# Layer 1 attention on one core: a head's 1280 scores taken in one piece instead of three

## The chip, the core and the metric

The kernel runs on one core of a Trainium2 chip. The metric is the device time of one execution in microseconds (us); the time of a kernel is the median of its timed runs. Engine names are those of the profile: PE is the matrix engine, DVE the vector engine, ACT the scalar engine, POOL and SP the two that mostly issue transfers here. Each engine runs its own instructions strictly in the order of the program and waits where an operand or a buffer is not ready.

## The reference

A two-layer network with a mixer and an expert layer in each layer. The change lies in the mixer of layer 1, in the dense attention of eight heads: 1024 query rows (8 tiles of 128) against 1280 keys (1024 of the sequence, 256 of a context).

```
def gqa_attend(q, k, v, mask, sink, scale):
    s = jnp.einsum('bqhgd,bkhd->bhgqk', q, k).astype(jnp.float32) * scale
    ...
    p = jax.nn.softmax(s, axis=-1)
    ...
    return jnp.einsum('bhgqk,bkhd->bqhgd', p.astype(v.dtype), v)
```

Behind the attention come an output projection (`y_lat`), the residual, a router (softmax over 16 experts for each token) and `lax.top_k(..., cap)` with cap = 128: each expert takes the 128 tokens with the highest router value. Then the experts run over the tokens gathered by these indices.

## The kernel before, in words

Every float32 operand of a matmul is split into a high and a low float16 part, and a product is three matmuls (`mm3`). The attention of layer 1 has 64 units of work, called heads below: 8 query tiles `t` times 8 heads `h`, taken in that order.

For each head `score(t, h, i)` writes the scores in three pieces `i` of 512, 512 and 256 keys (`KB`), three matmuls each, into a PSUM tile `sps` of one bank; five such banks rotate. DVE takes each piece's maximum (L1202). After the third piece DVE joins the three maxima and scales the result to `nm` (L1208, L1209). Then for each piece ACT forms the exponential `pr` with its row sum (L1218) and the high part (L112), and DVE the low part (L114); `pr` has two buffers. The parts are turned by a transposing transfer on SP's queue (`pT<-ps`, L147), the first piece by itself and the other two together. `values()` multiplies the turned parts with `vS` into `po`, thirty matmuls a head; after a tile's eighth head DVE divides by the row sums (`oc`, L1249) and the result is split and turned to `oT`.

Scores are taken `LA = 3` heads ahead of the values. Five streams are woven at build time by costs that each `yield` gives: `att_all` (this attention), `q_all` (the queries of the next tile), `tails`, `choose` and `splits`. A scheduler then fixes the order of every engine's instructions before the program runs; nothing is reordered on the chip.

`tails` first runs the convolution branch (`conv_all`, 576 matmuls into `cvps`) and the scaling of the output weights, and then, for each query tile whose `oT` is done, a tail: 48 matmuls into `yps`, two residual additions on DVE (`xx<-yps`, L301), a norm, eight transposes, sixteen router matmuls with a softmax, and a copy of the router values to `aff` (L334). A tail that is written after `att_all` has ended takes other PSUM tiles (`K["z"]`), which lie where the attention's stood.

`choose` waits for the fifth tail, then takes the 128 highest of the first 640 tokens for all experts at once in 16 rounds of three DVE instructions (`tkvr`, L350, L352, L354, 640 wide). After the eighth tail it does the same for the other 384 tokens (`tkvl`), merges both lists and writes `idxl` (L385), by which POOL gathers the experts' tokens.

Of the kernel before, what the change touches and what calls it, by code (L numbers as in the profile page):

```python
# [11 lines left out]
F32 = mybir.dt.float32  # L12
F16 = mybir.dt.float16
# [3 lines left out]
AF = mybir.ActivationFunctionType  # L17
OP = mybir.AluOpType
AX = mybir.AxisListType
# [3 lines left out]
P = 128  # L23
# [12 lines left out]
IS = 1.0 / WS  # L36
EPS = 1e-6
SC0 = 64.0 ** -0.5
SC1 = 96.0 ** -0.5
# [8 lines left out]
GR = ((0,), (1, 2))  # L48
# [29 lines left out]
class Net:  # L78
# [902 lines left out]
    def odd(self, ms, mw, xs, xsc, xd, h2d, W, then):  # L981
# [9 lines left out]
        if True:  # L991
# [109 lines left out]
            KB = ((0, 512), (512, 512), (1024, 256))  # L1101
            SP = ((), (0, 1), (2,))
# [6 lines left out]
            with self.pool("m1zp", PSUM) as pz:  # L1109
# [57 lines left out]
                if True:  # L1167
                    def Q(t):
                        qT = []
                        for i in range(2):  # L1170
# [5 lines left out]
                            S.activation(q, z, AF.Copy, scale=IS)  # L1176
# [14 lines left out]

                    def score(t, h, i):

                        qT, (c0, w) = K[t][h // 4], KB[i]
                        if i == 0:
                            K["mx"] = self.small.tile([P, 3], F32, name="mx3", bufs=3)
                            K["sp"] = []
                        mx, sp = K["mx"], K["sp"]
# [7 lines left out]
                        dn = self.small.tile([P, 3], F32, name="dn3", bufs=3)  # L1206
# [3 lines left out]
                        pTs = []  # L1210
                        for g, parts in enumerate(GR):
                            n = sum(KB[i][1] for i in parts)
                            ps = pt1.tile([P, 2, n], F16, name="ps1", tag=f"ps{g}", bufs=AB[1])
                            o = 0
                            for i in parts:
                                w = KB[i][1]
                                pr = pt1.tile([P, 512], F32, name="pr1", bufs=AB[0])
# [264 lines left out]
```

## Time and profile before

| what | value |
|---|---|
| median of 3 runs | 2640.53 us (2639.13 to 2646.84) |
| the profiled execution | 2632.11 us, of which the span is 2630.0 us |
| busy over the span | PE 89%, DVE 76%, ACT 65% |
| first scores of layer 1 attention | about 1503 us from the span's start |
| last convolution matmuls | about 1733 us |
| last value matmuls, then `oc` of the last tile | 1937.48 us |
| `idxl` written | 2025.36 us |

The profiled execution is 8.4 us below the median of the timed runs. Busy PE means that matmuls were under way, not that the array was at its peak. The layer 1 attention and the convolution beside it reach from 1503 to 1938 us, and the choice of tokens ends at 2026 us; the rest of the span, layer 0 ahead and the experts of layer 1 behind, is not touched by the diff.

### The profile page before, as it was taken

How to read it: one execution, taken by the hardware profiler on the slowest of the kernel's cores; microseconds unless marked ns; L12 is line 12 of the kernel's file. 1: busy time of each engine (PE TensorE's matmuls, PEld its weight loads, DVE VectorE, ACT ScalarE, POOL GpSimd, SP SyncE). 2: the span in 40 equal slices, each digit the busy share in tenths (PEclk: the TensorE clock that was granted, in tenths of full speed). 3: DMA queues.
4: the chain of work that ended last, by engine and by line, in shares of the span. 5: the costliest groups of instructions: out<-in, count | busy, mean ns of one | idle time of the engine just before them, and what ended most of it. 6: DMA issues, size and time to landing. Idle time of an engine off the chain costs nothing. (4 is left out here: it accounts for less than half of the span.)

```text
span 2630.0 us, 48132 instructions
## 1 busy us (share of the span) xinstructions
PE 2329.2 (89%) x19023; PEld 1415.0 (54%) x19023; DVE 1997.7 (76%) x3586; ACT 1696.7 (65%) x2748; POOL 320.6 (12%) x196
## 2 busy tenths in 40 slices
PE   6889998867999999999969999978982999999995
PEld 2335555543877778786836555535541444444442
DVE  5546767787887788777848687788796889888887
ACT  4434666535777787777726466567655777777774
POOL 1000000003111111111310000000025011112120
PEclk9999999877999999999989999989985999999998
DMA  8783555548998989888967577788866899999997
GB/s 321 192 213 84 134 104 116 123 126 312 352 337 324 328 328 325 327 320 300 326 187 203 119 143 143 133 151 184 176 175 272 311 364 395 368 360 367 361 363 274
DMA packets 461705, 660.25 MB, mean 251 GB/s; under 512 B 371083, under 2 KB 371387, under 8 KB 410789
## 3 DMA queue, kind: packets, MB, share of 16 engines
q1 hardware_dynamic: 439894, 582.81, 69.7%
q0 software_dynamic: 21584, 74.37, 9.8%
q8 instruction: 149, 2.44, 0.4%
q14 instruction: 78, 0.64, 0.1%
HBM read 525.82 MB, written 41.94 MB: 216 GB/s over the span
## 5 line engine op out<-in xcount | busy, mean ns | idle before, releaser
L101 DVE SCALAR_TENSOR_TENSOR spl<-raw,spl 128x2048 f16<-128x2048 f32 x369 | 834.6, 2285 | 167.3 <-ACT spl L100 166.5
L100 ACT ACTIVATE spl<-raw 128x2048 f16<-128x2048 f32 x369 | 693.5, 1911 | 166.4 <-DMA raw<-in_w 109.5
L141 PE MATMUL pa<-xsh,spl 128*128 128x160 f16 x1024 | 214.6, 233 | 2.3 <-ACT xsh L112 2.3
L143 PE MATMUL pb<-xsh,spl 128*128 128x160 f16 x1024 | 214.6, 233 | 0.5 <-DVE spl L101 0.5
L142 PE MATMUL pa<-xsl,spl 128*128 128x160 f16 x1024 | 214.7, 233 | 0.3 <-DVE xsl L114 0.3
L143 PE MATMUL pa<-xsh,spl 128*128 128x160 f16 x1024 | 214.7, 233 | 0.0
L142 PE MATMUL pb<-xsl,spl 128*128 128x160 f16 x1024 | 214.6, 233 | 0.0
L141 PE MATMUL pb<-xsh,spl 128*128 128x160 f16 x1024 | 214.5, 233 | 0.0
L141 PEld LDWEIGHTS <-spl 128*128 128x128 f16 x2048 | 200.6, 98 | 8.9 <-issue 8.0
L141 PE MATMUL y<-spl,gh 128*128 128x512 f16 x512 | 195.2, 384 | 9.0 <-ACT gh L112 8.4
L143 PEld LDWEIGHTS <-spl 128*128 128x128 f16 x2048 | 200.8, 98 | 1.1 <-DVE spl L101 0.7
L142 PEld LDWEIGHTS <-spl 128*128 128x128 f16 x2048 | 200.8, 98 | 0.3
L143 PE MATMUL y<-spl,gl 128*128 128x512 f16 x512 | 190.1, 386 | 11.4 <-DVE gl L114 11.3
L142 PE MATMUL y<-spl,gh 128*128 128x512 f16 x512 | 195.6, 382 | 1.8 <-DVE spl L101 1.8
L594 POOL DMA_INDIRECT xd<-ysb,idxl x31 | 113.2, 3652 | 532.3 <-DVE ysb L587 508.2
L1218 ACT ACTIVATE pr<-sps,nm 128x512 f32<-128x512 f32 (+1 forms) x192 | 116.7, 611 | 88.3 <-DVE nm L1209 67.7
L141 PE MATMUL po<-vS,pT 128*128 128x64 f16 x976 | 118.0, 198 | 49.1 <-DMA pT<-ps 32.5
L1201 PE MATMUL sps<-kT,qT 128*128 128x512 f16 (+1 forms) x576 | 134.4, 355 | 12.3 <-ACT pr L1218 11.9
L114 DVE TENSOR_TENSOR ps<-pr,ps 128x512 f16<-128x512 f32 (+1 forms) x192 | 112.2, 595 | 38.9 <-ACT ps L112 38.3
L141 PEld LDWEIGHTS <-pT 128*128 128x128 f16 x976 | 92.1, 101 | 82.8 <-DMA pT<-ps 46.5
L1202 DVE TENSOR_REDUCE mx<-sps 128x1 f32<-128x512 f32 (+1 forms) x192 | 112.8, 595 | 26.2 <-PE sps L1201 24.9
L208 PE MATMUL modps<-mslab,cs 128*2 128x512 f32 x384 | 88.5, 690 | 33.6 <-DMA mslab<-in_mod_w 28.7
(431 smaller groups left out, 5883.8 us busy)
## 6 DMA issues: line engine op xcount, KB each, us to landing
raw<-in_w SPq DMA_DIRECT2D x384, 1024.0 KB, 6.8
mslab<-in_mod_w SPq DMA_DIRECT2D x80, 512.0 KB, 4.8
mslab<-in_mod_w SPq DMA_DIRECT2D x8, 1024.0 KB, 8.2
raw<-in_wz SPq DMA_DIRECT2D x12, 512.0 KB, 6.4
raw<-in_wconv SPq DMA_DIRECT2D x24, 256.0 KB, 3.8
xin<-in_x POOLq DMA_DIRECT2D x8, 512.0 KB, 4.8
raw<-in_ev_wo SPq DMA_DIRECT2D x8, 512.0 KB, 6.9
xres<-in_x POOLq DMA_DIRECT2D x8, 512.0 KB, 5.4
```

What stands on the lines that cost most here:

```text
L100: self.S.activation(hi, raw, AF.Copy, scale=scale)
L101: self.V.scalar_tensor_tensor(lo, raw, scale, hi, op0=OP.mult, op1=OP.subtract)
L114: return self.V.tensor_tensor(lo, src, hi, OP.subtract)
L141: self.T.matmul(ps, lh, rh, start=first, stop=False)
L142: self.T.matmul(ps, lh, rl, start=False, stop=False)
L143: return self.T.matmul(ps, ll, rh, start=False, stop=last).ins
L208: T.matmul(ps[c0:c0 + 2], lhs, slab[:rows, g * 512:(g + 1) * 512], start=False, stop=(k == 8), tile_position=(0, c0))
L594: G.indirect_dma_start(out=xd, out_offset=IOA(ap=lat[0][:, e:e + 1], axis=0), in_=ysb, in_offset=None, compute_op=OP.add)
L1201: T.matmul(ps[:, :w], qT[:, 4 * j + h % 4], kT[:, k, c0:c0 + w], start=j == 0, stop=j == 2)
L1202: V.tensor_reduce(mx[:, i:i + 1], ps[:, :w], axis=AX.X, op=OP.max)
L1218: S.activation(pr[:, :w], sp[i][:, :w], AF.Exp, bias=nm, scale=SC1, accum_out=dn[:, i:i + 1])
```

## The change

The 1280 scores of a head lie side by side in PSUM. One tile of 2560 columns (five banks) holds two heads: even heads take columns 0 to 1279, odd heads 1280 to 2559. The third bank is shared: its first half belongs to the even head, its second half to the odd one. The odd head's pieces are 256, 512 and 512 keys, so that no piece crosses a bank. One DVE instruction takes the maximum over 1280 columns and negates it; the factor `SC1` moves into the copy of the queries. One ACT instruction forms the exponential of 1280 columns with its row sum straight into `rd`, one ACT instruction the high part, one DVE instruction the low part. `pr` becomes one buffer of 1280 columns. Two turns of five blocks each follow once both parts are there. `values()` works in two groups of five blocks, and for each head the attention's stream yields 0.6 three times and 0.3 twice, 2.4 in all, where it was 2.7.

```
-            KB = ((0, 512), (512, 512), (1024, 256))
-            SP = ((), (0, 1), (2,))
+            KB = ((0, 512), (512, 512), (1024, 256)), ((0, 256), (256, 512), (768, 512))
+            SP = (0, 1), (2,)
...
-                            S.activation(q, z, AF.Copy, scale=IS)
+                            S.activation(q, z, AF.Copy, scale=IS * SC1)
...
+                    two = pp.tile([P, 2560], F32, name="sps1")
+
                     def score(t, h, i):
 
-                        qT, (c0, w) = K[t][h // 4], KB[i]
...
-                        ps = pp.tile([P, 512], F32, name="sps1", tag="s", bufs=AB[4])
+                        n = (8 * t + h) % 2
+                        qT, (c0, w) = K[t][h // 4], KB[n][i]
+                        ps = two[:, 1280 * n:1280 * n + 1280]
                         for j, k in enumerate((h, h, 8)):
-                            T.matmul(ps[:, :w], qT[:, 4 * j + h % 4], kT[:, k, c0:c0 + w], start=j == 0, stop=j == 2)
-                        V.tensor_reduce(mx[:, i:i + 1], ps[:, :w], axis=AX.X, op=OP.max)
-                        sp.append(ps)
-                        if i < len(KB) - 1:
+                            T.matmul(ps[:, c0:c0 + w], qT[:, 4 * j + h % 4], kT[:, k, c0:c0 + w], start=j == 0, stop=j == 2)
+                        if i < len(KB[n]) - 1:
                             return
...
                         nm = self.small.tile([P, 1], F32, name="nm1", bufs=3)
-                        V.tensor_reduce(nm, mx, axis=AX.X, op=OP.max)
-                        V.tensor_scalar(nm, nm, -SC1, None, op0=OP.mult)
...
-                                pr = pt1.tile([P, 512], F32, name="pr1", bufs=AB[0])
-                                S.activation(pr[:, :w], sp[i][:, :w], AF.Exp, bias=nm, scale=SC1, accum_out=dn[:, i:i + 1])
-                                self.split_a(pr[:, :w], ps[:, 0, o:o + w], ps[:, 1, o:o + w])
...
+                        V.tensor_reduce(nm, ps, axis=AX.X, op=OP.max, negate=True)
...
-                        V.tensor_reduce(K["rd", t][:, h:h + 1], dn, axis=AX.X, op=OP.add)
+                        pr = pt1.tile([P, 1280], F32, name="pr1", bufs=1)
+                        S.activation(pr, ps, AF.Exp, bias=nm, accum_out=K["rd", t][:, h:h + 1])
+                        pf = pt1.tile([P, 2, 2, 640], F16, name="ps1", bufs=AB[1])
+                        prg = pr.rearrange("p (g c) -> p g c", g=2)
+                        self.split_a(prg, pf[:, :, 0], pf[:, :, 1])
+                        pTs = []
+                        for g in range(2):
+                            pT = pt1.tile([P, 2, 5, P], F16, name="pT1", tag=f"pT{g}", bufs=AB[2])
+                            self.turn(pT.rearrange("p s b c -> p (s b) c"), pf[:, g].rearrange("p s c -> p (s c)"))
+                            pTs.append(pT)
                         K["p", t, h] = pTs
```

The scheduler makes a new order of all that runs in this stage. Up to the first scores of layer 1 the order of every engine is the same in both programs. Line numbers shift: the maximum is L1203, the exponential L1207, the parts L111 and L113, `oc` L1233, `xx<-yps` L300, the copy to `aff` L333 and the first instruction of a top-k round L349 in the changed program.

The first place is DVE in the last heads, with `mx` the maximum, `ps<-pr` the low part of a head (each head with a number of its own). Before:

```order
L1202 TENSOR_REDUCE mx_24770<-sps_24806 128x1
L301 SCALAR_TENSOR_TENSOR xx<-yps,xx 128x512
L1202 TENSOR_REDUCE mx_24770<-sps_24845 128x1
L114 TENSOR_TENSOR ps_24727<-pr_24728,ps_24727 128x512
L1208 TENSOR_REDUCE nm_24851<-mx_24770 128x1
L114 TENSOR_TENSOR ps_24734<-pr_24735,ps_24734 128x512
L1202 TENSOR_REDUCE mx_24900<-sps_24901 128x1
L1209 TENSOR_SCALAR nm_24851<-nm_24851 128x1
```

Here the maxima of the next head (24770, 24900) stand among the low parts of the head ahead of it (24727, 24734). The same place in the changed program, down to the end of the attention:

```order
L1203 TENSOR_REDUCE nm_23493<-sps_18971 128x1
L113 TENSOR_TENSOR ps_23497<-pr_23495,ps_23497 128x2x640
L1203 TENSOR_REDUCE nm_23557<-sps_18971 128x1
L113 TENSOR_TENSOR ps_23561<-pr_23559,ps_23561 128x2x640
L1203 TENSOR_REDUCE nm_23619<-sps_18971 128x1
L1231 RECIPROCAL rd<-rd 128x8
L113 TENSOR_TENSOR ps_23623<-pr_23621,ps_23623 128x2x640
L1233 TENSOR_TENSOR oc<-po_23362,rd 128x512
L113 TENSOR_TENSOR oh<-oc,oh 128x512
L300 SCALAR_TENSOR_TENSOR xx<-yps,xx 128x512 x2
```

Now the low part of a head always stands ahead of the next head's maximum; so it is for 61 of the 63 pairs of neighbours in the whole stage.

On ACT likewise the exponential and the high part of a head (L1207, L111) now alternate with those of the next, one of each.

The second place is DVE where the choice of tokens begins. Before, its first round (`tkvr`) stands among the low parts of the last two heads:

```order
L1202 TENSOR_REDUCE mx_24981<-sps_25018 128x1
L334 COPY aff<-affps 16x128
L1208 TENSOR_REDUCE nm_25024<-mx_24981 128x1
L350 MAX tkvr<-aff 16x8
L114 TENSOR_TENSOR ps_24938<-pr_24939,ps_24938 128x512
L1209 TENSOR_SCALAR nm_25024<-nm_25024 128x1
L114 TENSOR_TENSOR ps_24945<-pr_24946,ps_24945 128x512
L352 MAX_INDEX tkir<-tkvr,aff 16x8
```

After, 26 rows lie between the last head's low part and it, the residual additions of two and a half tails among them:

```order
L126 TENSOR_SCALAR rstdt<-rstt,rsyt 128x1
L300 SCALAR_TENSOR_TENSOR xx<-yps,xx 128x512
L333 COPY aff<-affps 16x128
L349 MAX tkvr<-aff 16x8
L351 MAX_INDEX tkir<-tkvr,aff 16x8
L353 MATCH_REPLACE aff<-tkvr,aff 16x640
L349 MAX tkvr<-aff 16x8
```

The third place is POOL's queue, which writes a tail's rows back (`xd<-xx`, `h<-xx`) and forms the low parts of expert slabs fetched ahead (`spl<-raw`); such a fetch begins when the attention has ended. Before (`xx_24873` is the fifth tail, the two after it the sixth and seventh):

```order
L306 DMA xd1_64<-xx_24873 128x1024
L336 DMA h21_66<-xx_24873 128x1024
L434 TENSOR_TENSOR spl_25666<-raw_25177,spl_25666 128x2048
L306 DMA xd1_64<-xx_25287 128x1024
L434 TENSOR_TENSOR spl_25670<-raw_25179,spl_25670 128x2048
```

After (`xx_23917` is the fifth tail, `xx_24072` the sixth):

```order
L433 TENSOR_TENSOR spl_24451<-raw_23813,spl_24451 128x2048
L305 DMA xd1_64<-xx_23917 128x1024
L433 TENSOR_TENSOR spl_24455<-raw_23815,spl_24455 128x2048
L335 DMA h21_66<-xx_23917 128x1024
L433 TENSOR_TENSOR spl_24459<-raw_23817,spl_24459 128x2048
L305 DMA xd1_64<-xx_24072 128x1024
```

The fifth tail's two writes, ahead of the first slab before, now stand behind the first and the second slab. Its buffer `xx` is the one that the seventh tail loads into, since two buffers take turns.

The fifth tail is the one whose copy to `aff` opens the choice. In PE's order of before, the fifth tail's `yps` matmuls stand ahead of the last value matmuls, and 144 (three tails) behind them; in the changed program 192 (four tails) stand behind them, and 125 of these ahead of the transpose that delivers the fifth tail's router values. The convolution's 576 matmuls end in both programs when 33 heads are scored and 30 to 31 have their values. Between the scores of two neighbouring heads they come in lumps: 0 to 37 of them after the change.

## Rows read from the trace of the kernel before

**Rows 1.** The page's first part: busy us (share of the span), instructions.

```profile
PE 2329.2 (89%) x19023; PEld 1415.0 (54%) x19023; DVE 1997.7 (76%) x3586; ACT 1696.7 (65%) x2748; POOL 320.6 (12%) x196
```

**Rows 2.** Busy time of the engines in three stretches, clock, transfers.

```profile
core 0: us, PE busy (x) PEld busy (x) DVE busy (x) ACT busy (x) POOL busy (x), PEclk, DMA share, GB/s
1503.00:1733.00 230.00, 222.85 (x1926) 122.54 (x1925) 176.41 (x445) 146.16 (x364) 0.00 (x0) 1.00 0.73 138
1733.00:1938.00 205.00, 165.09 (x1628) 98.95 (x1625) 163.90 (x422) 140.84 (x343) 5.33 (x10) 0.91 0.87 172
1938.00:2026.00 88.00, 44.14 (x221) 25.48 (x220) 71.63 (x197) 53.76 (x45) 44.05 (x17) 0.71 0.62 248
```

**Rows 3.** The same stretches, matmuls into `po` alone: PE busy (count), DVE busy, clock.

```profile
1503.00:1733.00 230.00, 45.38 (x955) 2.04 (x3) 1.00 0.73 138
1733.00:1938.00 205.00, 47.61 (x972) 3.25 (x5) 0.91 0.87 172
```

**Rows 4.** DVE from 1895 us: start, us, operation (first round, last division, end of round 16).

```profile
1925.35 0.82 DVE L350 MAX8 tkvr<-aff 16x8 f32<-16x640 f32 x1
...
1937.48 0.69 DVE L1249 TENSOR_TENSOR oc<-po,rd 128x512 f32<-128x512 f32 x1 [0.56 <-PE po L143]
...
1974.39 0.23 DVE L360 TENSOR_SCALAR tkir<-tkir 16x128 f32<-16x128 uint32 x1
```

**Rows 5.** DVE from 1973 us: second top-k, indices.

```profile
1997.64 0.55 DVE L350 MAX8 tkvl<-aff 16x8 f32<-16x384 f32 x1
...
2025.36 0.17 DVE L385 CAST idxl<-slps 128x16 int32<-128x16 f32 x1 [0.49 <-PE slps L384]
```

**Rows 6.** Groups by shape, 1503 to 1938: busy, mean ns, idle ahead, releasers.

```profile
L1202 DVE TENSOR_REDUCE mx<-sps 128x1 f32<-128x512 f32 x128 | 87.2, 684 | 15.6 <-PE sps L1201 14.6
L1218 ACT ACTIVATE pr<-sps,nm 128x512 f32<-128x512 f32 x128 | 86.5, 680 | 70.0 <-DVE nm L1209 67.7 <-DVE ps L114 2.0
L114 DVE TENSOR_TENSOR ps<-pr,ps 128x512 f16<-128x512 f32 x128 | 85.7, 684 | 35.9 <-ACT ps L112 35.6
L112 ACT ACTIVATE ps<-pr 128x512 f16<-128x512 f32 x128 | 75.1, 625 | 0.3
...
L1218 ACT ACTIVATION_READ_ACCUMULATOR pr<-sps,nm 128x1 f32 x192 | 37.6, 196 | 0.0
...
L1218 ACT ACTIVATE pr<-sps,nm 128x256 f32<-128x256 f32 x64 | 30.1, 471 | 18.3 <-DVE ps L114 18.3
L1202 DVE TENSOR_REDUCE mx<-sps 128x1 f32<-128x256 f32 x64 | 26.7, 417 | 10.6 <-PE sps L1201 10.3
L114 DVE TENSOR_TENSOR ps<-pr,ps 128x256 f16<-128x256 f32 x64 | 26.6, 416 | 3.0 <-ACT ps L112 2.7
L112 ACT ACTIVATE ps<-pr 128x256 f16<-128x256 f32 x64 | 26.6, 415 | 1.7
L1208 DVE TENSOR_REDUCE nm<-mx 128x1 f32<-128x3 f32 x64 | 9.4, 148 | 0.4
```

**Rows 7.** The page's groups: the two parts of an expert slab, 2048 wide.

```profile
L101 DVE SCALAR_TENSOR_TENSOR spl<-raw,spl 128x2048 f16<-128x2048 f32 x369 | 834.6, 2285 | 167.3 <-ACT spl L100 166.5
L100 ACT ACTIVATE spl<-raw 128x2048 f16<-128x2048 f32 x369 | 693.5, 1911 | 166.4 <-DMA raw<-in_w 109.5
```

**Rows 8.** DVE and ACT around 1737 us: a hand-over from one to the other.

```profile
1737.25 0.14 DVE L1209 TENSOR_SCALAR nm<-nm 128x1 f32<-128x1 f32 x1
...
1737.43 0.69 ACT L1218 ACTIVATE pr<-sps,nm 128x512 f32<-128x512 f32 x1 [1.03 <-DVE nm L1209]
```

**Rows 9.** Transfers issued from 1733 to 1938: count, us from issue to landing.

```profile
pT<-ps SPq DMA_TRANSPOSE x64, 3.7
```

**Rows 10.** A window in which PE is half idle (columns as in rows 2).

```profile
1755.00:1780.00 25.00, 13.46 (x121) 6.88 (x120) 23.19 (x43) 18.32 (x39) 0.00 (x0) 0.72 0.80 174
```

**Rows 11.** Third stretch of rows 2, matmuls into `yps` alone: PE busy, DVE busy, clock.

```profile
1938.00:2026.00 88.00, 32.66 (x143) 3.95 (x6) 0.71 0.62 248
```

**Rows 12.** POOL from 1900 us: the low part of the second slab fetched ahead.

```profile
1957.02 4.08 POOL L434 TENSOR_TENSOR spl<-raw,spl 128x2048 f16<-128x2048 f32 x1 [2.27 <-ACT spl L433]
```

More of the change, by code (lines that the diff above doesn't have):

```diff
@@ L47 @@
 AB = (2, 2, 3, 0, 5, 1)
-GR = ((0,), (1, 2))
 LA = 3
@@ L1190, in Q @@
                             yield 0.5
+                    two = pp.tile([P, 2560], F32, name="sps1")
                     def score(t, h, i):
-                        qT, (c0, w) = K[t][h // 4], KB[i]
[L1195 to L1198, printed above, removed]
-                        ps = pp.tile([P, 512], F32, name="sps1", tag="s", bufs=AB[4])
+                        n = (8 * t + h) % 2
+                        qT, (c0, w) = K[t][h // 4], KB[n][i]
+                        ps = two[:, 1280 * n:1280 * n + 1280]
@@ L1205, in score @@
                             return
-                        dn = self.small.tile([P, 3], F32, name="dn3", bufs=3)
                         nm = self.small.tile([P, 1], F32, name="nm1", bufs=3)
-                        V.tensor_reduce(nm, mx, axis=AX.X, op=OP.max)
-                        V.tensor_scalar(nm, nm, -SC1, None, op0=OP.mult)
[L1210 to L1216, printed above, removed]
-                                pr = pt1.tile([P, 512], F32, name="pr1", bufs=AB[0])
-                                S.activation(pr[:, :w], sp[i][:, :w], AF.Exp, bias=nm, scale=SC1, accum_out=dn[:, i:i + 1])
-                                self.split_a(pr[:, :w], ps[:, 0, o:o + w], ps[:, 1, o:o + w])
-                                o += w
-                            pT = pt1.tile([P, 2, n // P, P], F16, name="pT1", tag=f"pT{g}", bufs=AB[2])
-                            self.turn(pT.rearrange("p s b c -> p (s b) c"), ps.rearrange("p s c -> p (s c)"))
-                            o = 0
-                            for i in parts:
-                                w = KB[i][1] // P
-                                pTs.append(pT[:, :, o:o + w])
-                                o += w
@@ L1237, in values @@
                         t, h, i, pT = pend.pop(0)
-                        c0, w = KB[i]
                         if (h, i) == (0, 0):
@@ L1241, in values @@
                         po = K["po", t]
-                        for b in range(w // P):
-                            vb, vs = c0 // P + b, slice(h * 64, h * 64 + 64)
+                        for b in range(5):
+                            vb, vs = 5 * i + b, slice(h * 64, h * 64 + 64)
                             self.mm3(po[:, h], pT[:, 0, b], pT[:, 1, b], vS[:, vb, 0, vs], vS[:, vb, 1, vs], vb == 0, vb == 9)
-                        if (h, i) == (7, len(KB) - 1):
+                        if (h, i) == (7, 1):
                             rd = K["rd", t]
@@ L1261, in att_all @@
                             pTs = K.pop(("p", t, h))
-                            for i in range(len(KB)):
+                            for i in range(2):
                                 pend.append((t, h, i, pTs[i]))
```

## The prediction, made before the changed kernel ran

> **What bounds the kernel now.** The whole-kernel shares [rows 1] call no engine full: PE is busy for 89% of the span. So I cut the stage that the change touches into three stretches [rows 2]. From the first scores at 1503 us to the end of the convolution at 1733 us PE is busy 222.85 of 230 us, DVE 176.41 and ACT 146.16: this stretch is PE's, because the convolution fills what the attention leaves free. From 1733 to 1938 us PE is busy 165.09 of 205 us, DVE 163.90, ACT 140.84. There nobody is full, and the time is made of waits between the three engines. The value matmuls count the heads [rows 3]: 955/30 = 31.8 heads in the first stretch, 7.2 us each; 972/30 = 32.4 in the second, 6.3 us each.
>
> The third stretch, 1938 to 2026 us, is another matter. DVE is busy 71.63 of 88 us with the choice of tokens. Its first top-k starts at 1925.35 us, 12 us before the last head's result is divided at 1937.48 us, and ends at 1974.39 us [rows 4], 49 us with what runs in between. The second top-k starts at 1997.64 us, when the eighth tail is through, and the indices stand at 2025.36 us [rows 5], 27.7 us later. So the first top-k is hidden now: it has 23 us to spare before the second needs it.
>
> **The work that goes.** A head's vector work is read by dividing groups by 64 [rows 6]. DVE: maxima (87.2+26.7)/64 = 1.78 us, low parts (85.7+26.6)/64 = 1.76 us, three small operations of 0.15 us, in all 3.98 us. ACT: exponentials (86.5+30.1)/64 = 1.82 us, three reads of the sum 37.6/64 = 0.59 us, high parts (75.1+26.6)/64 = 1.59 us, in all 4.00 us.
>
> No operation on 1280 columns is in the trace. I extend each from its two nearest sizes. The maximum goes from 417 ns at 256 columns to 684 ns at 512, 1.04 ns a column, so 0.684 + 768 x 0.00104 = 1.48 us. The exponential: 0.680 + 768 x 0.00082 = 1.31 us. The low part, from 684 ns at 512 to 2285 ns at 2048 columns [rows 6, 7]: 1.48 us; the high part, from 625 to 1911 ns: 1.27 us. From below, the bound is no fixed cost left at all; from above, three times the pieces now; I take the straight line, since 2048 columns lie on the far side. With one read of the sum at 0.20 us a head costs DVE 2.96 us and ACT 2.78 us. That is 1.0 and 1.2 us less a head, 65 and 78 us over the stage. Matmuls, turned bytes and the 128 turns stay as they are, so PE has the same work.
>
> The Trainium skill's page Perfetto Trace Analysis, section Optimizing Scalar/DVE Operations, says that grouping into larger operations helps when the engine is saturated, and that breaking instructions up can get work done sooner where it is not saturated but makes others wait. By its first half the sum would be that of the faster case below, by its second half this change loses. The trace agrees with the condition of the second half: in the second stretch DVE is at 80% and ACT at 69%, and PE waits.
>
> **The wait that comes.** Before, a head's three pieces let DVE and ACT work on two heads at once. Now the orders shown ahead leave one chain: exponential, high part, low part, the next head's maximum, the next exponential. The single `pr` says the same: its next writer waits for the low part. The chain is 1.31 + 0.20 + 1.27 + 1.48 + 1.48 = 5.74 us a head; hand-overs between engines cost some 0.04 us (0.14 us from 1737.25, then 1737.43 [rows 8]), and neighbours on one engine overlap by as much. PE hides in it: a head's nine score matmuls must wait for the exponential ahead, since both heads share the third bank, but they need only be done by the end of the low part.
>
> The same Trainium skill page, section Matmuls, wants independent matmul groups to rotate through different PSUM banks so that reading one overlaps writing the next. The trace of before shows only five banks in turn; no row shows a shared bank, and in my sum it costs nothing by itself.
>
> To the chain comes every other instruction that stands inside it in the order: on DVE between a low part and the next maximum, on ACT between an exponential and its high part, and what does not fit between. Bounds: none, or all other work. In the first stretch that is 176 - 31.8 x 3.98 = 50 us on DVE and 146 - 31.8 x 4.00 = 19 us on ACT; in the second 35 and 11 us. Counting places in the order, a little over half stands inside: 39 us in the first stretch, 27 us in the second.
>
> First stretch: 32 heads x 5.74 + 39 = 223 us of chain, against 223 us of PE work. The two bounds are equal, and PE's filler comes in lumps of 0 to 37 convolution matmuls between the scores of two heads: where a lump is long the chain waits, where there is none PE does. Taking each head's longer side gives 241 us, the longer total 223 us; now it is 230 us. I take 234: **+4 us** (-7 to +11).
>
> Second stretch: 31 heads from score to score, 31 x 5.74 + 27 = 205 us, then the last head's maximum, exponential, parts, turn and values, 1.5 + 1.5 + 1.3 + 1.5 + 3.7 [rows 9] + 1 = 10.5 us: 215 us against 205. In the last eleven heads PE has nothing else to do. Where PE is busy 13.46 of 25 us the granted clock is 0.72 [rows 10], and score matmuls at the lower of the two levels take longer than the slack of about 1 us; that adds 0 to 10 us, I take 3. **+13 us** (0 to +20).
>
> **What is late next.** In the new order the fifth tail stands behind the attention. Its router values open the first top-k, which therefore starts after the last head and no longer 12 us before. From the end of the values: 125 `yps` matmuls at 32.66/143 = 0.228 us [rows 11] are 28.5 us, with transposes and softmax 30 us. But DVE's order has the seventh tail's first addition ahead of the copy that starts the top-k, and the seventh tail's rows load into the fifth tail's buffer, whose last write stands on POOL behind the second slab. That slab's low part takes 4.08 us from 1957.02 [rows 12], so it ended 24 us after the attention; a write and a load at 4 to 5 us each make 33 to 35 us. Then 49 us as now, then 27.7 us: 34 + 49 + 27.7 = 111 us, against 2025.36 - 1937.48 = 88 us. **+23 us**; +14 us if the clock is full and no load is late, +32 us if one more slab stands ahead. The prefetched slabs begin at the end of the attention and shift with it; the experts behind keep their work.
>
> **Sum.** 4 + 13 + 23 = +40 us on 2632.1 us, 2672 us for a profiled run. That run was 8.4 us under the median, so the median goes from 2640.5 to **2680 us**. With the bounds, -7+0+14 = +7 to 11+20+32 = +63 us.
>
> **Rivals.**
> *The chain is covered.* PE and DVE keep today's pace in both stretches, only the top-k is late: +14 to +32 us, 2655 to 2672 us. For it speaks that half of the chain's extra work might fall where DVE would idle anyway; against it the strict alternation.
> *The top-k stays hidden.* The second top-k waits for the eighth tail, not for the first top-k, and loses only the fifth tail's 10.9 us (48 x 0.228): 17 + 11 = +28 us, or as little as 0 to +10 us if the attention also holds. Against it: 34 + 49 us is past the 60 us at which the second begins now.
> *Faster.* The lighter engines win: no other instruction delays the chain, the second stretch takes 31 x 5.74 + 10.5 = 188 us (-17) and the first loses PE's idle 7 us. That is -24 us, and it decides only from the point where the late top-k costs less: at +14 it is -10 us, 2630 us.
> *Worse than forecast.* DVE and PE wait for each other in their queues (an addition that needs `yps` stands in the chain while PE waits for an exponential), 1 us more for half of the heads: +70 us, 2710 us.
>
> **Chances.** Forecast 0.55, chain covered 0.17, top-k hidden 0.12, faster 0.08, worse 0.08. No change that can be told is within 0.3%, 8 us: a small part of the hidden top-k and of the covered chain, and half of the faster case. So faster 0.06, same 0.08, slower 0.86. The range leaves out the faster case below and the worse one above: 2648 to 2708 us.
>
> **What would show it.** Right, step by step: the 1280-column operations near 1.48 us on DVE and 1.3 us on ACT; ACT idle before the exponential, released by the maximum, in nearly every head, and PE idle before `sps`, released by the exponential; about 6.5 us a head behind the convolution; `tkvr` starting some 34 us after the last `oc`, and the second top-k directly behind the first. Wrong: the last `oc` before 1930 us, a first top-k that starts within 20 us of it, or 1280-column operations under 1.2 us, which would take 1 us from every head.

## The result, and the profile after

The changed kernel takes 2724.3 us (median of 4 runs, 2722.8 to 2733.7) against 2640.8 us of the kernel before in the same job: ratio 1.032, 95% interval 1.029 to 1.035. The forecast was 2680 us, 2648 to 2708: slower as forecast, but by 83 us where 40 were forecast. The two profiled executions differ by 92 us (spans 2722.2 and 2630.0), since that of before was 8.4 us under its median.

First the page of the changed kernel: busy us by engine [rows 1], and the 1280-wide groups that replace those of [rows 6].

```profile
PE 2364.6 (87%) x19023; PEld 1434.7 (53%) x19023; DVE 1973.8 (73%) x3138; ACT 1646.5 (60%) x2364; POOL 307.2 (11%) x196
...
L1207 ACT ACTIVATE pr<-sps,nm 128x1280 f32<-128x1280 f32 x64 | 84.9, 1326 | 186.8 <-DVE nm L1203 182.3
...
L113 DVE TENSOR_TENSOR ps<-pr,ps 128x1280 f16<-128x1280 f32 x64 | 95.4, 1490 | 77.1 <-ACT ps L111 76.3
L1199 PE MATMUL sps<-kT,qT 128*128 128x512 f16 (+1 forms) x576 | 135.5, 388 | 17.1 <-ACT pr L1207 16.8
L1203 DVE TENSOR_REDUCE nm<-sps 128x1 f32<-128x1280 f32 x64 | 95.2, 1487 | 42.0 <-PE sps L1199 41.5
```

The work that goes is as forecast: maximum and low part are (95.2 + 95.4)/64 = 2.98 us a head on DVE, where 2.96 were forecast and 3.98 stood before. ACT is 50 us less busy over the span, DVE 24 (the page counts overlapping neighbours once, and short operations overlap more), and the kernel is slower all the same. ACT is idle 187 us ahead of the exponentials (88 before, [rows 6]).

Next the busy times by stage of the changed kernel, as in [rows 2], cut at its own marks: first score, last convolution matmul, last `oc`, indices.

```profile
1514.10:1771.50 257.40, 228.76 (x1885) 124.25 (x1886) 156.96 (x209) 121.15 (x166) 0.00 (x0) 0.95 0.64 119
1771.50:2005.70 234.20, 170.05 (x1592) 102.74 (x1589) 141.21 (x178) 113.50 (x148) 4.27 (x8) 0.85 0.71 148
2005.70:2119.00 113.30, 58.33 (x294) 33.21 (x292) 90.41 (x226) 58.58 (x53) 48.94 (x19) 0.73 0.55 216
```

The same cut of the kernel before. Its last convolution matmul ends at 1724.7 us; the 1733 us given ahead of the prediction are the last convolution operation on DVE:

```profile
1503.40:1724.70 221.30, 215.17 (x1841) 117.96 (x1842) 168.52 (x424) 140.02 (x350) 0.00 (x0) 1.00 0.73 136
1724.70:1937.50 212.80, 172.06 (x1709) 103.38 (x1706) 171.23 (x443) 146.57 (x357) 5.33 (x10) 0.92 0.87 174
1937.50:2025.40 87.90, 44.32 (x221) 25.30 (x219) 71.53 (x195) 53.76 (x45) 43.86 (x16) 0.71 0.62 248
```

So the attention takes 491.6 us from first score to last division where it took 434.1 (+36.1 with the convolution, +21.4 behind it), and division to indices takes 25.4 us more. Behind the indices 603 us are left (605 before). The first score stands 10.7 us later; the program ahead of it is the same, and in the profiles of the runs below, the one built on the kernel before among them, it starts between 1503 and 1522 us. That part is spread between executions.

What PE waited for tells where the 57 us lie. Waits of the changed kernel from 1514 to 2006 us (total us, times, longest):

```profile
ACT pr L1207 <- DVE nm L1203: 182.3, 54, 5.7
...
PE po L140 <- DMA pT<-ps: 71.4, 40, 7.9
DVE nm L1203 <- PE sps L1199: 41.5, 29, 3.8
...
PE sps L1199 <- ACT pr L1207: 16.8, 12, 3.0
```

The same from 1503 to 1938 us in the kernel before:

```profile
PE po L141 <- DMA pT<-ps: 32.5, 31, 3.0
...
DVE mx L1202 <- PE sps L1201: 24.9, 33, 2.0
...
PE sps L1201 <- ACT pr L1218: 11.9, 11, 4.1
```

The value matmuls wait 39 us longer for their turned parts, DVE waits 17 us longer for scores, and PE works at a lower clock (0.95 and 0.85 for 1.00 and 0.92). One head shows how this reaches the chain; rows of DVE, PE and ACT in the changed kernel:

```profile
1939.35 1.49 DVE L113 TENSOR_TENSOR ps<-pr,ps 128x1280 f16<-128x1280 f32 x1 [0.72 <-ACT ps L111]
...
1944.75 0.23 PE L140 MATMUL po<-vS,pT 128*128 128x64 f16 x1 [2.11 <-DMA pT<-ps]
...
1945.47 1.49 DVE L113 TENSOR_TENSOR ps<-pr,ps 128x1280 f16<-128x1280 f32 x1 [1.10 <-ACT ps L111]
...
1945.55 2.80 PE L1199 MATMUL sps<-kT,qT 128*128 128x512 f16 x9
...
1948.38 1.49 DVE L1203 TENSOR_REDUCE nm<-sps 128x1 f32<-128x1280 f32 x1 [1.42 <-PE sps L1199]
```

The low part of one head ends at 1940.84; its first turn lands at 1944.7, and 15 value matmuls that read it stand ahead of the scores of the head after next on PE. Those scores, 2.80 us long at a low clock, end at 1948.35, 1.4 us after DVE is free. From low part to maximum: 3.9 + 0.8 + 2.8 us, then 1.5 + 1.5 + 1.3 + 1.5 us to the low part of the head after next: 13.3 us for two heads, 6.65 a head, where the chain alone has 5.76.

The top-k, as in [rows 4, 5]: first round of the first top-k, last round, first round of the second, indices.

```profile
2037.87 0.82 DVE L349 MAX8 tkvr<-aff 16x8 f32<-16x640 f32 x1
...
2083.70 0.81 DVE L349 MAX8 tkvr<-aff 16x8 f32<-16x640 f32 x1
...
2085.43 0.53 DVE L349 MAX8 tkvl<-aff 16x8 f32<-16x384 f32 x1
...
2119.04 0.17 DVE L384 CAST idxl<-slps 128x16 int32<-128x16 f32 x1 [0.48 <-PE slps L383]
```

It starts 32 us after the last `oc` (2005.72), and the second follows directly, as forecast.

### The profile page after: what moved, and what is told of

It reads as the page before. It is cut to its first block, busy times and chain, and to the rows that moved or that the text cites. A ratio compares the mean times of both kernels' runs of the same rounds, so it can differ in the third digit from the quotient of the medians.

```text
span 2722.2 us, 47217 instructions
## 1 busy us (share of the span) xinstructions
PE 2364.6 (87%) x19023; PEld 1434.7 (53%) x19023; DVE 1973.8 (73%) x3138; ACT 1646.5 (60%) x2364; POOL 307.2 (11%) x196
## 5 line engine op out<-in xcount | busy, mean ns | idle before, releaser
L1207 ACT ACTIVATE pr<-sps,nm 128x1280 f32<-128x1280 f32 x64 | 84.9, 1326 | 186.8 <-DVE nm L1203 182.3
L593 POOL DMA_INDIRECT xd<-ysb,idxl x31 | 106.9, 3449 | 555.4 <-DVE ysb L586 528.2
L113 DVE TENSOR_TENSOR ps<-pr,ps 128x1280 f16<-128x1280 f32 x64 | 95.4, 1490 | 77.1 <-ACT ps L111 76.3
L1199 PE MATMUL sps<-kT,qT 128*128 128x512 f16 (+1 forms) x576 | 135.5, 388 | 17.1 <-ACT pr L1207 16.8
L1203 DVE TENSOR_REDUCE nm<-sps 128x1 f32<-128x1280 f32 x64 | 95.2, 1487 | 42.0 <-PE sps L1199 41.5
```

The costliest lines, as they stand in the source:

```text
L113: return self.V.tensor_tensor(lo, src, hi, OP.subtract)
L593: G.indirect_dma_start(out=xd, out_offset=IOA(ap=lat[0][:, e:e + 1], axis=0), in_=ysb, in_offset=None, compute_op=OP.add)
L1199: T.matmul(ps[:, c0:c0 + w], qT[:, 4 * j + h % 4], kT[:, k, c0:c0 + w], start=j == 0, stop=j == 2)
L1203: V.tensor_reduce(nm, ps, axis=AX.X, op=OP.max, negate=True)
L1207: S.activation(pr, ps, AF.Exp, bias=nm, accum_out=K["rd", t][:, h:h + 1])
```

## The experiments

Seventeen kernels, each timed against the kernel before. Medians are compared with the 2724 us of the changed kernel, which they edit unless said otherwise. The kernel before came to 2638.9 to 2644.8 us in these jobs, so a difference of a few us tells nothing. "PE's waits" are those for a turn and for an exponential from first score to last division (71 and 17 us in the changed kernel, 33 and 12 before).

**e1, values later.** Each value matmul is issued behind the last score of head n+2.

```diff
+with self.behind(K["sm", min(n + 2, 8 * NT - 1)].ins):
     values()
```

> Only the order on PE differs from the changed kernel: the value matmuls of head n stand behind the scores of head n+2, so that they are a full head further behind the turn they read (2.0 heads behind the scores throughout; 1.0 to 2.0 in the changed kernel, mostly 2.6 in the kernel before). Theory A, the scores are late because they queue behind value matmuls that wait for their turned parts: the gaps ahead of the maximum that follow such a wait add up to some 23 us in the changed kernel's trace, and the time falls by 15 to 25 us, to 2699 to 2709 us; the waits of po for pT fall from 71 us to under 20. Rival B, the chain of exponential, parts and maximum sets the pace alone, as the prediction had it, and whatever PE waits for is hidden: within 6 us of 2724.

2700.3 us, -24: theory A by the number. But the waits only half agree. From 1507 to 1978 us:

```profile
PE sps L1199 <- ACT pr L1207: 62.6, 30, 5.3
...
PE po L140 <- DMA pT<-ps: 10.5, 10, 3.9
```

The wait for the turn falls from 71 to 10.5 us, and 46 us more of waiting for an exponential have come. The attention falls by 20 us to 471, not to 434. Its first two stretches:

```profile
1507.20:1758.10 250.90, 225.17 (x1880) 123.08 (x1881) 157.25 (x209) 120.97 (x166) 0.00 (x0) 0.97 0.64 122
1758.10:1978.50 220.40, 164.50 (x1594) 98.99 (x1592) 141.04 (x177) 113.22 (x148) 4.28 (x8) 0.87 0.78 158
```

Behind the convolution it is 8 us over the kernel before (21 in the changed kernel), with the convolution still 30 (36).

**e2, fifth tail early.** `yield 0.6` behind a score becomes `yield 0.7`.

> The attention's steps count 0.7 and not 0.6 in the interleaving, as many units a head as in the kernel before (2.7 against 2.4). In the built order 144 and not 192 yps matmuls stand behind the last value matmul and the first round of the top-k stands ahead of the last division again, as in the kernel before. Theory A, the late fifth tail costs the 25 us by which last division to indices grew (113 us, 88 before): that stretch falls back to 86 to 92 us and the time to 2700 to 2710 us, since the fifth tail's 11 us of matmuls are taken up in the attention in part. Rival B, the late top-k is a consequence of the long attention and not of this order: that stretch stays over 105 us and the time within 8 us of 2724.

2697.3 us, -27; division to indices 90.0 us. The attention stays at 492 us with the fifth tail in it. Theory A, 3 us under its range.

**e3, maximum first.** The high and low part and the turns of a head are issued behind the next head's maximum.

```diff
+mi = V.tensor_reduce(nm, ps, axis=AX.X, op=OP.max, negate=True)
+if K.get("parts"):
+    with self.behind(mi.ins):
+        K.pop("parts")()
```

> The high and low part of a head are issued behind the next head's maximum, so that DVE's order is maximum of n+1, low part of n in all heads (in two of 63 in the changed kernel); the value matmuls come out 2.0 heads behind the scores with it. One buffer for the exponentials as before. Theory A, strict turn taking on one chain of 5.74 us sets the pace: with the maximum out of the chain the chain is exponential, high part, low part, 4.3 us, and the time from the first to the last head's exponential falls from 478 us by 50 to 90 us, less where PE is the bound in the convolution stretch; 2640 to 2680 us in all. Rival B, PE's scores are the bound, since a head's scores wait for the exponential ahead in the shared bank and the maximum can't start earlier: the maximum then only delays the low part, and the time is 2724 us or more. Rival C, only the values' order of the first run counts: equal to that run.

2785.3 us, +61: rival B. Rows of ACT, PE and DVE:

```profile
2032.13 1.33 ACT L1210 ACTIVATE pr<-sps,nm 128x1280 f32<-128x1280 f32 x1 [4.36 <-DVE ps L113]
...
2033.60 2.78 PE L1199 MATMUL sps<-kT,qT 128*128 128x256 f16 x9 [2.65 <-ACT pr L1210]
2036.48 1.49 DVE L1203 TENSOR_REDUCE nm<-sps 128x1 f32<-128x1280 f32 x1 [4.45 <-PE sps L1199]
2037.89 1.48 DVE L113 TENSOR_TENSOR ps<-pr,ps 128x1280 f16<-128x1280 f32 x1
2039.47 1.33 ACT L1210 ACTIVATE pr<-sps,nm 128x1280 f32<-128x1280 f32 x1 [4.62 <-DVE ps L113]
```

The chain here is exponential, all nine scores, maximum, low part: 7.3 us a head. In this kernel a head's scores do not begin before the exponential of the head ahead has ended.

**e4, two buffers** for the exponentials (`pr1` with `bufs=2`).

> The buffer of the exponentials is there twice (room made by letting q and oc, and qq and oh, share buffers). DVE's order still has the low part of n ahead of the maximum of n+1, now in all heads. Theory A, the order on DVE makes the chain, the single buffer adds nothing to it: in the heads behind the convolution the time from one exponential to the next stays over 6 us, and the time within 12 us of 2724. Rival B, the single buffer is what makes the chain: the exponential no longer waits for the low part, 1.49 us less a head, 64 x 1.49 = 95 us less, 2630 us.

2702.5 us, -22, outside both. Behind the convolution a head still takes 7.4 us (maxima at 1820.04 and 1967.27, 20 heads), so the order and not the buffer sets the pace there. But the built order put 43 heads, not 33, into the convolution's stretch, and the attention came to 476 us. The first score was at 1503.1 us, 11 us earlier than in the changed kernel, so part of the 22 us may be spread.

**e5, both orders** of e1 and e2.

> Both orders of the first two runs at once: the value matmuls behind the scores of head n+2, and the attention's steps at 0.7, so that the fifth tail stands inside the attention again. Theory A, the two costs are apart and add up: 2724 - 24 - 27 = 2673 us, 2665 to 2685; what is left over the kernel before, some 30 us, is the chain itself with the other work inside it. Rival B, both cure the same wait (PE finds something to do while it waits for a turn): 2690 to 2700 us.

2705.2 us, -19: neither, and not better than either alone. PE's waits are 19 and 55 us, the attention 499.5 us with the fifth tail in it. That e1's order exchanges one wait for the other explains that nothing adds up; why it comes out 8 us over e2 stays open.

**e6, shared piece last.** In odd heads the 256 columns in the bank that both heads use are scored last.

```diff
-((0, 256), (256, 512), (768, 512))
+((256, 512), (768, 512), (0, 256))
```

> In odd heads the 256 columns in the bank that both heads share are scored last and not first, so that 6 of 9 score matmuls no longer wait for the exponential ahead (in even heads they stand last already). Orders on the engines else as in the changed kernel. Theory A, in the changed kernel's order the scores have the time of both parts, 2.76 us, after an exponential, so the shared bank costs only what PE shows as waiting for it, 17 us in all with half of it for odd heads: 2712 to 2724 us. Rival B, the shared bank delays every second head by the time of 6 matmuls, 1.1 to 2 us: 32 x 1.5 = 48 us less, 2676 us.

2727.2 us, +3: rival B falls by the number, but the edit does not free the 6 matmuls. In its trace, as in that of the changed kernel, no score matmul starts before the exponential of the head ahead has ended, those in other banks included. So this run does not say what a shared bank costs.

**e7 and e8, own banks.** The block gets 3072 columns, three banks for each head; the convolution, the queries and the tails share one bank in place of two. e7 has the maximum first, as e3; e8 has not.

```diff
-zc, zt = Tag(pz, "zc", 1), Tag(pz, "zt", 1)
+zc = zt = Tag(pz, "zc", 1)
-two = pp.tile([P, 2560], F32, name="sps1")
+two = pp.tile([P, 3072], F32, name="sps1")
```

> As e3_max_first, but each head has three banks of its own (the convolution and the tails get one bank in place of two for it). Theory A, in e3_max_first the shared bank put the scores and the maximum on the chain (exponential, scores, maximum, low part, exponential); with own banks the scores run under the exponential and the chain is exponential, high part, low part, 4.3 us, plus other work: over 90 us less than e3_max_first, 2650 to 2695 us. Rival B, it was the maximum ahead of the low part in itself that cost time, since the low part, the turn and the values come later by it: over 2750 us.

> Each head has three banks of its own, the convolution and the tails one in place of two; DVE still has the low part ahead of the maximum. The control for e7_max_first_own_banks. Theory A, with this order on DVE the chain of 5.74 us stays and the shared bank costs little by itself, while the convolution's single bank costs some: 2712 to 2745 us. Rival B, the shared bank is the main cost of the change, whatever the order: under 2690 us.

2784.5 us (e3: 2785.3) and 2726.7 us, +2. In e7 theory A fell: own banks changed nothing. The built programs say why. `two` is one tile with two halves, and all scores of head n wait for the exponential of head n-1, whichever bank they write; in both traces none of the 567 score matmuls behind the first head starts before that exponential has ended. So these two do not test the shared bank by itself either.

**e9, two tiles** of three banks.

```diff
-two = pp.tile([P, 2560], F32, name="sps1")
+two = [pp.tile([P, 1536], F32, name="sps1", tag=f"s{n}", bufs=1) for n in range(2)]
```

> The two halves of the PSUM block become two tiles, three banks each (the convolution and the tails keep one bank). In the built program the scores of head n then wait for the exponential of head n-2; with one tile, in the changed kernel and in e8_own_banks too, all of a head's scores wait for that of head n-1, also those in banks of their own. DVE's order comes out with the maximum of n+1 ahead of the low part of n in 52 of 63 heads, the values mostly 3 heads behind the scores. Theory A, the one tile is what makes the chain: the waits of PE for a turn and for an exponential (72 and 17 us in the changed kernel, 33 and 12 before) fall together below those of the kernel before, and first score to last division falls from 492 us to 440 or less; the tails stand further back in this order (240 of 384 matmuls behind the last value matmul), which gives some back: 2650 to 2690 us in all. Rival B, the chain is in the wide operations themselves and their one buffer: attention over 480 us, over 2715 us.

2668.0 us, -56, and 59 under e8, from which it differs by the tiles and the order that was built with them (50 heads and not 33 are scored by the end of the convolution). Theory A. Here 434 of the 567 score matmuls start before the exponential of the head ahead has ended. First score to last division is 417 us. Its waits from 1519 to 1937 us, and four exponentials of one token tile:

```profile
ACT pr L1207 <- DVE ps L113: 59.8, 40, 4.2
DVE nm L1203 <- PE sps L1199: 46.9, 17, 9.9
...
PE po L140 <- DMA pT<-ps: 25.6, 24, 5.7
```

```profile
1531.64 1.32 ACT L1207 ACTIVATE pr<-sps,nm 128x1280 f32<-128x1280 f32 x1
1535.97 1.33 ACT L1207 ACTIVATE pr<-sps,nm 128x1280 f32<-128x1280 f32 x1 [1.62 <-DVE ps L113]
1540.31 1.33 ACT L1207 ACTIVATE pr<-sps,nm 128x1280 f32<-128x1280 f32 x1 [1.62 <-DVE ps L113]
1544.65 1.33 ACT L1207 ACTIVATE pr<-sps,nm 128x1280 f32<-128x1280 f32 x1 [1.62 <-DVE ps L113]
```

4.33 us a head: exponential, high part, low part, with the maximum out of the chain. Inside a token tile the scores are now early, and the exponential waits for the low part where it waited for the maximum. DVE still waits 46.9 us for scores, but in 17 long waits. Division to indices is 143 us, as 240 matmuls of the tails stand behind the attention.

**e10 and e11**, e9 with the attention's steps at 0.9 and 1.2.

> As e9_two_tiles, with the attention's steps at 0.9 in the interleaving: 96 yps matmuls behind the last value matmul, the top-k's first round 41 rows ahead of the last division on DVE. Theory A: attention as long as in e9_two_tiles plus the tails it takes in (some 30 us), the stretch from last division to indices back at or under 88 us: 2620 to 2655 us, at or below the kernel before. Rival B: 2690 us or more.

> As e9_two_tiles, with the attention's steps at 1.2: the convolution ends after 32 scored heads, 48 yps matmuls stand behind the last value matmul. Theory A: PE stays full longest here, 2605 to 2650 us, below the kernel before. Rival B, the convolution's single bank and the late heads take it back: 2650 us or more.

2695.1 and 2743.6 us: rival B in both. The top-k is early (83 and 62 us to the indices), but the attention grows to 500 and 557 us.

**e12, the kernel before with three banks** for scores: `AB[4]` from 5 to 3.

> The kernel before with three PSUM banks for scores in place of five: pieces of 512 and 256 columns as there, but a head's scores can only start as the exponentials of the head ahead free their banks. The built order has the values 1.0 to 1.6 heads behind the scores, as the changed kernel has, and the fifth tail in its old place. Theory A, the lost head of lookahead is the main cost of the change, whatever the width of the operations: the waits of po for the turn rise from 33 us to 60 or more and the time by 25 to 60 us, to 2666 to 2700. Rival B, the wide operations make the cost: within 8 us of 2641.

2747.0 us against 2638.9 in that job: ratio 1.039, interval 1.034 to 1.043. Less lookahead alone, in the old kernel with its narrow operations, costs 108 us, nearly twice the upper end of what I expected: theory A in its direction, outside it in size. Waits from 1514 to 2063 us, and the stretch behind the convolution (212.8 us before):

```profile
PE po L141 <- DMA pT<-ps: 94.0, 55, 4.8
...
DVE mx L1202 <- PE sps L1201: 51.3, 44, 3.4
```

```profile
1767.90:2063.10 295.20, 209.37 (x1741) 119.94 (x1742) 212.02 (x517) 151.83 (x369) 5.33 (x10) 0.79 0.62 129
```

**e13 and e14, e9 with the tails in**: steps at 0.8, queries at rate 20; e14 with the second buffer too.

> As e9_two_tiles, with the attention's steps at 0.8 and the queries interleaved earlier, so that 145 yps matmuls stand behind the last value matmul (144 in the kernel before, 240 in e9). Theory A, with the lookahead back the lighter vector work is worth little, since PE's matmuls and the turns bound the stage: first score to indices 510 to 540 us (522 in the kernel before, 560 in e9), 2630 to 2660 us in all. Rival B, the 2.2 us a head that DVE and ACT save come out in full once the wait is gone: under 500 us, under 2615 us. Rival C, the single bank for convolution, queries and tails costs what the lookahead gives: over 550 us, over 2670 us.

> As e13, with the buffer of the exponentials twice (q and oc, qq and oh share buffers). Built order: values 3.5 to 4 heads behind the scores within a token tile, 144 yps matmuls behind the last value matmul. Theory A: within 10 us of e13, since the exponential's wait for the low part falls mostly where PE is the bound. Rival B, the single buffer is the next limit (exponentials wait for the low part 60 us in e9): 20 us or more below e13.

2704.8 and 2722.2 us: rival C for e13. First score to indices takes 591 us in e13. Inside a token tile most heads take 4.3 to 5 us, but from a tile's eighth head to the next tile's first it is up to 50 us. ACT waits for `qps` and `cvps`, which share the one bank, but only 10 and 5 us in all; so that the single bank makes these heads late is not shown. The second buffer made it 17 us worse, not better, outside both ideas for e14.

**e15 to e17, 1024 and 256.** Five banks as before, two again for the others: a tile of 1024 columns with two buffers and one of 256 with one. Two maxima and two exponentials a head, one high and one low part. Steps at 0.6, 0.7 and 0.8.

```diff
+if i == 0: K["a"] = pp.tile([P, 1024], F32, name="sps1", tag="a", bufs=2)
+elif i == 2: K["b"] = pp.tile([P, 256], F32, name="spt1", tag="b", bufs=1)
...
+V.tensor_reduce(mx[:, 1:2], K["b"], axis=AX.X, op=OP.max)
+V.tensor_reduce(mx[:, 0:1], K["a"], axis=AX.X, op=OP.max)
+V.tensor_reduce(nm, mx, axis=AX.X, op=OP.max, negate=True)
...
+S.activation(pr[:, 1024:], K["b"], AF.Exp, bias=nm, accum_out=dn[:, 1:2])
+S.activation(pr[:, :1024], K["a"], AF.Exp, bias=nm, accum_out=dn[:, 0:1])
```

> Scores of a head in a tile of 1024 columns (two buffers) and one of 256 (one buffer), five banks as in the kernel before; maxima and exponentials in two pieces, high and low part in one; one buffer for the exponentials. The attention's steps at 0.6 as in the changed kernel; 192 yps matmuls stand behind the last value matmul. Theory A, the lookahead decides: no loss of 15 to 50 us every eighth head, attention under 430 us with fewer tails in it, top-k late as in the changed kernel: 2625 to 2660 us. Rival B, waits at every token tile stay: over 2680 us.

> As e15, steps at 0.7; 144 yps matmuls behind the last value matmul, as in the kernel before. Theory A, attention at or under the 434 us of the kernel before, first score to indices 500 to 530 us: 2615 to 2650 us. Rival B: over 2670 us.

> As e15, steps at 0.8; 96 yps matmuls behind the last value matmul. Theory A: within 15 us of e16 on either side. Rival B, the heads of the last token tiles come late as they did at 0.9 with two tiles: 30 us or more over e16.

2630.0, 2621.9 and 2649.7 us; ratios to the kernel before 0.996 (0.995 to 0.998), 0.993 (0.991 to 0.995) and 1.003 (1.001 to 1.004). Theory A in e15 and e16, which beat the kernel before by 0.4% and 0.7%; e17 is 28 us over e16, outside theory A and just short of rival B. In e17 the attention is 28 us longer than in e16 and the indices come 20 us sooner behind it, but 23 us more pass behind the indices; why stays open. The stages of e16, and its wait for the turn from 1490 to 1950 us:

```profile
1513.20:1762.70 249.50, 243.38 (x2239) 137.45 (x2240) 198.62 (x362) 156.69 (x281) 0.00 (x0) 0.99 0.83 149
1762.70:1921.30 158.60, 133.48 (x1283) 80.80 (x1281) 115.40 (x220) 92.69 (x162) 4.27 (x8) 0.95 0.83 178
1921.30:2019.00 97.70, 46.52 (x246) 28.41 (x244) 86.64 (x224) 58.56 (x53) 48.94 (x19) 0.72 0.62 243
```

```profile
PE po L140 <- DMA pT<-ps: 17.5, 17, 5.5
```

PE is full to 98% in the first stretch, its clock is back, and first score to indices is 505.8 us for 522.0. With the lookahead kept, the kernel with the lighter vector work is some 16 us shorter here; how much of it is the work and how much the new order (43 heads scored by the end of the convolution, 33 before) is not separated, and the steps alone move the time by 28 us.

## Why the prediction was wrong

**Sizes of operations: right.** Forecast 1.48, 1.31, 1.48, 1.27 and 0.20 us; measured 1.487, 1.326, 1.490, 1.266 and 0.192. The straight lines, from 256 and 512 columns for maximum and exponential and from 512 and 2048 for the parts, held to 0.02 us.

**The chain: right as a mechanism.** Exponential to exponential adds up to 5.76 us of work, 5.74 forecast. ACT's idle time ahead of the exponentials ends with the maximum in 54 of 64 heads, as the prediction had it. e9 shows the same chain without the maximum, 4.33 us. But from the first exponential to the last a head takes 7.59 us on the mean.

**The step that failed** is in "The wait that comes": "PE hides in it: a head's nine score matmuls must wait for the exponential ahead, since both heads share the third bank, but they need only be done by the end of the low part." PE did not hide. DVE waited 41.5 us for scores, 23.5 with the convolution and 18.0 behind it, where the sum had 11 (234 for 223) and 3 for what PE adds. The sign that the prediction gave for this step, PE idle before `sps` until the exponential, came in 12 of 64 heads, 16.8 us: in most heads something else stood ahead of the scores in PE's queue.

Behind the convolution that was matmuls of the tails (`yps`) and in good part value matmuls whose turns had not landed. By PE's rows these run 1.0 to 2.0 heads behind the scores (1.6 on the mean) where in the kernel before they run mostly 1.7 to 2.7 (2.2), and I had not counted that. e1 takes this wait away and gives back 14 of the 21 us there. With the convolution it was mostly convolution matmuls: in the 21 heads whose scores end after the low part ahead of them, PE ran these for 47 us between the exponential and the scores and was idle for a turn for 4. I had these lumps and counted too little for them; e1 gives back only 6.5 of the 36 us. This part is read from rows; no run moved the convolution alone.

What both have in common in the changed kernel is that no score starts before the exponential of the head ahead has ended, so that whatever delays PE delays the chain. PE's idle time with the convolution is 6.1 us before, 28.6 in the changed kernel, 25.7 in e1, and 6.1 again in e16, where the scores can run ahead. e9 takes 56 us off by two tiles, and e12 makes the loss in the old kernel. The reason given in the step was wrong too: the wait comes from the one tile, since it stays with own banks in e7 and e8. What the shared bank costs by itself no run shows. The Trainium skill's page Perfetto Trace Analysis, section Matmuls, asks for different banks for independent groups. Here banks alone gave nothing, since the program waits by tile.

By terms: **+4** for the first stretch and **+13** for the second, +17 together, measured +57.5 (+34.9 and +22.6 by the prediction's mark, the last convolution operation on DVE, at 1732.9 and 1778.5 us). In the first stretch PE is idle for 29 us, 19 in waits for a turn and 8 for an exponential by its rows, and busy 13.6 us longer on nearly the same matmuls at 0.95 of the clock. I had the bounds from chain and PE side by side and chose between them; the kernel, 264 us by that mark, went past the upper (241 us). **+23** for the top-k: measured +25.4, and e2 takes it back. That it came so near is in part luck: its three parts are 32.2, 47.6 and 33.6 us for 34, 49 and 27.7, and the last holds an operation of 4 us described at the end. Ahead of the attention **0**: 10.7 us, spread. Behind the indices **0**: -1.4 us. The bounds of the sum add up to 2648 to 2704 us; the 2708 of the range stands in no sum.

**Rivals.** "Worse than forecast" priced this kind of wait, a mutual one between PE and DVE, at 1 us for half of the heads. It was nearest, and too small and too improbable at 0.08. "Faster" fell here; e16 is faster than the kernel before, but with another layout and order. e12 shows the loss without any wide operation and e16 wide operations without the loss; so the wide operations are not what cost the time.

## What to carry to other kernels

When a change joins buffers, count how many units of work the producer can be ahead, before and after, and see what stands ahead of it in its own queue: here the lost lookahead (five banks for 1.67 heads before, one tile that lets no score past the exponential ahead after) cost more than the lighter vector work gave back. Two halves of one tile are one buffer to a scheduler that tracks tiles, whatever banks they lie in. Join the operations whose operands already lie side by side (the two parts in SBUF), and leave the pieces in PSUM small enough to be buffered twice.

## What the hardware showed that was not expected

Nine score matmuls of the same sizes take 1.78 us in one head and 2.80 us (shown above) in another, 6 us apart, in a stretch where the granted clock is 0.85 on the mean. The clock was at its lower level, 0.50 (1.2 GHz), for most of the slow head and at 1.00 (2.4 GHz) in the fast one. First the scores of the fast head, then the stretch ahead of the slow head, its scores, and those of the fast one (columns as in [rows 2]):

```profile
1951.44 1.78 PE L1199 MATMUL sps<-kT,qT 128*128 128x256 f16 x9 [0.30 <-ACT pr L1207]
```

```profile
1943.00:1945.00 2.00, 0.25 (x5) 0.25 (x6) 0.20 (x1) 1.97 (x3) 0.00 (x0) 0.80 1.11 217
1945.00:1947.00 2.00, 2.00 (x18) 1.13 (x16) 1.49 (x1) 0.44 (x1) 0.00 (x0) 0.50 0.31 58
1951.00:1953.00 2.00, 1.70 (x14) 0.91 (x11) 0.28 (x1) 1.66 (x3) 0.00 (x0) 1.00 0.23 43
```

Ahead of the slow head PE had waited 2.11 us for a turn and was busy for 0.25 of 2 us; in the chain that 1 us comes on top of the wait. That the wait caused it is not shown: ahead of the fast head PE had waited 1.74 us, and the clock stayed. In e12 the clock behind the convolution fell to 0.79, in e16, where PE waits less, it was 0.95.

A second thing fell on the top-k. A DVE operation that takes 0.23 us in the kernel before (the end of its round 16, [rows 4]) took 4.01 us while POOL made a slab's low part. A second one, ahead of it, took 2.16 us in the same company. Rows of DVE and POOL in the changed kernel:

```profile
2081.63 2.16 DVE L326 TENSOR_SCALAR re<-re,rden 128x16 f32<-128x16 f32 x1
...
2085.89 4.01 DVE L359 TENSOR_SCALAR tkir<-tkir 16x128 f32<-16x128 uint32 x1
```

```profile
2079.70 4.05 POOL L433 TENSOR_TENSOR spl<-raw,spl 128x2048 f16<-128x2048 f32 x1 [2.02 <-ACT spl L432]
2085.78 4.05 POOL L433 TENSOR_TENSOR spl<-raw,spl 128x2048 f16<-128x2048 f32 x1 [2.02 <-ACT spl L432]
```

Each ends with the low part beside it, at about 2083.8 and 2089.85 us. It is the same in the traces of all nineteen kernels together: of the operations of these two kinds (a `TENSOR_SCALAR` of 128x16 elements, or of 16x128 from integers), 49 began inside a low part on POOL and all 49 ended with it, up to 4.02 us long; the 369 others took 0.32 us at most. The rounds of the top-k do not show it: the replacement at 2080.90 us took 0.80 us inside the first of these low parts. The Trainium skill's page GPSIMD Engine Reference, section Specifications, says that GpSimd's SBUF interfaces are shared with VectorE, with contention for some of its instructions. These rows agree with that.
